# A fused hybrid decoder layer: four plain feed-forward pairs in place of five, six of their eight weight splits kept for the second token half, h2 kept whole, and the last splits tied into a chain

## The chip, the cores and the metric

The kernel runs on one core of one Trainium2 chip. The metric is the device time of one launch in microseconds (us). Three runs of the kernel before gave 939.48, 940.89 and 943.55 us; the median is 940.89 us. TensorE is called PE, VectorE DVE, ScalarE ACT, GpSimd POOL and SyncE SP, as in the profile.

## The reference, cut to what matters

One layer: a gated mixer (attention, gMLP, projections), and then a SwiGLU feed-forward block on 512 prompt tokens and 8 sample tokens (520 in all), with D_MODEL 1024 and D_FF 2816 (22 tiles of 128). The change lies in the last two lines and in the norm ahead of them.

```python
def trunk_layer(x, c, attend, sgu, w_ada, b_ada, norm1_w, w_in, ..., w_out, norm2_w, w_ffn_in, w_ffn_out):
    ...
    x = x + g1 * (merged @ w_out)
    h2 = rms_norm(x, norm2_w) * (1 + sc2) + sh2
    a, b = jnp.split(h2 @ w_ffn_in, 2, axis=-1)
    x = x + g2 * ((jax.nn.silu(a) * b) @ w_ffn_out)
    return x, att_state, vs
```

## The kernel before

Everything is stored with features on the 128 partitions and the 520 tokens in the free dimension, in two halves of 260 (`HT`). Each float32 operand of a large product is split in two float32r parts: `hi`, a rounding copy made by ACT (L68), and `lo`, the rest, made by DVE (L69). A product then takes three matmuls per block of 128 features (`mm3`, L91 to L93: hi·hi, hi·lo, lo·hi), each 128x128 by 260 columns. A weight tile of 1024x128 against one token half is a `product` of 8 blocks, 24 matmuls.

The whole kernel is a list of jobs. `run()` walks it: `steps()` loads a weight tile with SP, splits it on ACT and DVE into a ring of three buffers for `hi` and three for `lo`, and keeps three splits ahead of the products; after each job `tick()` advances the background tasks (norms, sums) by a piece. What comes out is then ordered per engine by a scheduler with a cost model of its own, so an instruction's place on its engine isn't simply its place in the text. PE has four PSUM banks under the tag `mm`, used in turn; a product can start only when the bank's last reader is done.

The stages that matter here, in order of time:

- The out projection, token half by token half (`out_job`, 8 products each); DVE adds each product to the residual (`residual`, L837, for the second half also `rt` and `xr` on the 8 sample tokens, L841 and L842).
- `norm2(half)`, a background task of each half: squares on ACT, sums mostly on POOL, a sum over features by one PE matmul (`tot`, L296), then Ln, Exp and a Newton step (`rsqrt`), and for each of 8 blocks `modulate`: a product on DVE (L277), h2 `hi` on ACT (L279), h2 `lo` on DVE (L280). For the first half it runs beside the second half's out products, for the second half beside the first half's plain feed-forward products.
- The plain feed-forward tiles (`ffn_job`): `NPRE` = 5 tile pairs, gate and value, first all 10 products of the first token half, then all 10 of the second, each time with its weights loaded and split anew. The gate product goes through Silu on ACT (L905), the value product is multiplied with it on DVE (L908).
- `sums()`, a background task in the second half's plain products: it rebuilds h2 as hi + lo (`whole`, L927), and forms differences of its four quarters (L930); three of them go split into `tt`, and the fourth, `t1`, is written over the second half of the first four blocks of h2 once the plain products have read them (ACT L933, DVE L930).
- The other 17 tiles are pairs (`pair_job`). A pair takes seven part products of 12 matmuls, 84 in all, on sums and differences of weights (formed by POOL in `first`, L974 and L975, and by DVE, L990 and L993) and of h2 quarters, where a plain tile pair takes 4 products, 96 matmuls. The first part of each pair (`start_pair`) stands in the pair before; those of the first pair stand at its own start, 24 matmuls ahead of the first use of `t1`.
- The down projection (`down_job`, 8 output tiles, three k ranges). Its operands are the 22 gated tiles, split by `divide` (also L68 and L69): tiles 0 and 1 during the last pairs, 2 to 7 during the last pair into the space of `tt`, 8 to 15 into that of h2, the rest later. `g` L1031 is the last step of a pair, and it frees the pair's bank `pa`.

Of the kernel before, what the change touches and what calls it, by code (L numbers as in the profile page):

```python
# [1 line left out]

# [8 lines left out]
F32 = mybir.dt.float32  # L11
F32R = mybir.dt.float32r
# [15 lines left out]
TILES = {1: 1, 2: 3}  # L28
# [3 lines left out]
def hybrid_layer(ctx: ExitStack, tc: tile.TileContext, io: dict):  # L32
# [88 lines left out]
    def job(src, fn, n=KD):  # L121

        def prep(raws):
            yield weights(*raws[0])

        def use(ops, after):
            fn(*ops[0])
            yield

        jobs.append(([(src, n)], None, prep, use))  # L130

    def run():
# [6 lines left out]
        def loads():  # L139
            while len(raws) < len(jobs):  # L140
                srcs, first = jobs[len(raws)][:2]
# [7 lines left out]
        def steps():  # L149
            for k, (_, _, prep, _) in enumerate(jobs):  # L150
                loads()
                for op in prep(raws[k]):
# [10 lines left out]
        for k, (_, _, _, use) in enumerate(jobs):  # L163
            parts = use(ops[k], ops[k + 1] if k + 1 < len(jobs) else None)
            n = TILES[len(jobs[k][0])]
            for p in range(n):
# [3 lines left out]
                next(step, None)  # L170
# [102 lines left out]
    def modulate(which, f, x, rstd, c0, c1, hi, lo):  # L273
# [7 lines left out]
                                 in1=hi[:, c0:c1].bitcast(F32), op0=ALU.add, op1=ALU.subtract)  # L281

    def modulate_samples(which, f0, n, x, rstd, h):
# [7 lines left out]
        last_h[0] = split(h[:, fs, TP:T], h[:, f0 + KD : f0 + KD + n, TP:T], t)  # L291

# [539 lines left out]
    xr, h2, xr_all, h2_all = [], [], [], []  # L832
# [11 lines left out]
    def norm2(half):  # L844
# [15 lines left out]
        if half == 0:  # L860
            h2_all.append(slots("h", "h2", 2 * KD, F32R))
            h2.extend((h2_all[0][1][f], h2_all[0][1][KD + f]) for f in range(KD))
            scales(1, 0, KD, n2w)
        else:
            modulate_samples(1, 0, KD, xr_all[0][0], rstd2, h2_all[0][0])
        for f in range(KD):
            modulate(1, f, xr[f], rstd2, half * HT, min(half * HT + HT, TP), *h2[f])
# [24 lines left out]
    gs, pend, mem = {}, {}, {}  # L892
# [7 lines left out]
    def ffn_job(i, which, half):  # L900
        def fn(hi, lo):
            p = product(hi, lo, h2, half)
            if which == 0:
# [6 lines left out]
        job(io["wff"][which * NFF + i], fn)  # L910
# [5 lines left out]
    def sums():  # L916

        early.close()
        tt = ctx.enter_context(tc.tile_pool(name="tt", bufs=1)).tile([P, 3, KD, HT], F32R, tag="tt", name="tt")
        mem["tt"] = tt  # L920
        mem["ys"] = slots("ys", "g8")
# [292 lines left out]
```

## Time and profile before

| what | us |
|---|---|
| median of three runs (lowest, highest) | 940.89 (939.48, 943.55) |
| the profiled execution, its own time | 938.87 |
| its span, first to last instruction | 936.7 |
| PE busy in the span | 910.1 (97%) |
| DVE, ACT, POOL busy | 585.3 (62%), 413.1 (44%), 136.0 (15%) |
| feed-forward and down part, from the first plain product to the end | 570.6 to 936.7 |

The page gives busy time per engine, the span in slices, and the costliest groups. In a timeline row the first number is the start, the second the length, and the bracket is the idle time of the engine just before it with what ended it; matmuls overlap, so the time that one costs is the distance between two starts, not its length.

### The profile page before, as it was taken

Reading aid. Unit: us, or ns where it says so; the run is one execution under the profiler, and the core shown is the slowest. Engines: PE = TensorE matmul, PEld = TensorE weight load, DVE = VectorE, ACT = ScalarE, POOL = GpSimd, SP = SyncE. Lnnn points to the kernel's source line nnn. Section 1 sums busy time; section 2 is a strip of 40 time slices with the busy share of each in tenths; the row PEclk is TensorE's granted clock in tenths of the full one; section 3 lists DMA queues with packets and bytes.
Section 4 is the critical chain, followed back from the end, with each engine's and each line's share of the span. In section 5 each row is a group of like instructions: output and inputs, shape, how many; then the busy total and the mean of one; then the engine's idle time right before and its main releaser. Section 6 shows DMA issues by size and latency. Waiting matters only on the chain. (4 is left out here: it accounts for less than half of the span.)

```text
span 936.7 us, 18863 instructions
## 1 busy us (share of the span) xinstructions
PE 910.1 (97%) x7648; PEld 870.7 (93%) x7648; DVE 585.3 (62%) x1378; ACT 413.1 (44%) x802; POOL 136.0 (15%) x155
## 2 busy tenths in 40 slices
PE   3899999999999999999999999999999999899998
PEld 1699889899898989999999999999999999899998
DVE  6734675746655665643337678998887887742321
ACT  4343443533543443763333356664555556622110
POOL 0000002012102102201000322022343342000000
PEclk9999999999999999999999999999999999999999
DMA  9944436738758636635222654542332332343410
GB/s 358 360 160 136 159 113 230 265 97 301 241 175 255 221 98 180 225 111 161 91 91 90 227 180 156 181 159 91 121 106 91 113 113 91 103 143 95 119 40 23
DMA packets 43030, 146.85 MB, mean 157 GB/s; under 512 B 6456, under 2 KB 7448, under 8 KB 42944
## 3 DMA queue, kind: packets, MB, share of 16 engines
q1 hardware_dynamic: 33840, 114.34, 36.1%
q0 software_dynamic: 8608, 31.20, 10.7%
q8 instruction: 60, 0.98, 0.4%
q14 instruction: 26, 0.21, 0.1%
q10 hardware_dynamic: 496, 0.12, 0.1%
HBM read 137.01 MB, written 8.63 MB: 155 GB/s over the span
## 5 line engine op out<-in xcount | busy, mean ns | idle before, releaser
L91 PE MATMUL ps<-h,hi 128*128 128x260 f32 x1248 | 354.7, 287 | 3.1 <-ACT h L279 2.1
L93 PE MATMUL ps<-h,lo 128*128 128x260 f32 x1248 | 353.4, 285 | 0.6 <-DVE lo L69 0.6
L92 PE MATMUL ps<-h,hi 128*128 128x260 f32 x1248 | 353.3, 284 | 0.3 <-DVE h L280 0.3
L69 DVE TENSOR_TENSOR lo<-raw,hi 128x1024 fp32r<-128x1024 f32 (+2 forms) x213 | 220.0, 1050 | 163.3 <-ACT hi L68 161.1
L68 ACT ACTIVATE hi<-raw 128x1024 fp32r<-128x1024 f32 (+2 forms) x213 | 181.5, 875 | 256.2 <-PE ps L92 215.4
L91 PEld LDWEIGHTS ps<-h,hi 128*128 128x128 f32 x1248 | 233.7, 188 | 14.2 <-issue 9.1
L92 PEld LDWEIGHTS ps<-h,hi 128*128 128x128 f32 x1248 | 234.7, 188 | 3.3 <-issue 2.1
L93 PEld LDWEIGHTS ps<-h,lo 128*128 128x128 f32 x1248 | 234.8, 188 | 3.2 <-issue 1.7
L974 POOL TENSOR_TENSOR s<-raw 128x512 f32<-128x512 f32 x17 | 34.2, 2011 | 147.2 <-DMA raw<-wff 114.3
L953 PE MATMUL pb<-h,hi 128*128 128x260 f32 x136 | 38.9, 286 | 1.8 <-DVE h L930 1.8
L954 PE MATMUL pb<-h,lo 128*128 128x260 f32 x136 | 39.1, 287 | 0.0
L952 PE MATMUL pb<-h,hi 128*128 128x260 f32 x136 | 38.9, 286 | 0.0
L953 PE MATMUL pa<-tt,hi 128*128 128x260 f32 x136 | 38.6, 284 | 0.0
L91 PE MATMUL ps<-gh,hi 128*128 128x260 f32 x128 | 36.2, 283 | 2.5 <-DVE g L1031 2.5
L952 PE MATMUL pa<-tt,hi 128*128 128x260 f32 x136 | 38.6, 284 | 0.0
L954 PE MATMUL pa<-tt,lo 128*128 128x260 f32 x136 | 38.3, 282 | 0.0
L93 PE MATMUL ps<-mh,lo 128*128 128x260 f32 x128 | 36.3, 284 | 0.0
L91 PE MATMUL ps<-mh,hi 128*128 128x260 f32 x128 | 36.2, 283 | 0.0
L92 PE MATMUL ps<-ml,hi 128*128 128x260 f32 x128 | 36.2, 283 | 0.0
L92 PE MATMUL ps<-gh,hi 128*128 128x260 f32 x128 | 36.1, 282 | 0.0
L93 PE MATMUL ps<-gh,lo 128*128 128x260 f32 x128 | 36.1, 282 | 0.0
L837 DVE SCALAR_TENSOR_TENSOR xr<-ps,mod,xr 128x260 f32<-128x260 f32 (+1 forms) x32 | 15.4, 482 | 30.8 <-PE ps L93 29.9
(271 smaller groups left out, 1887.2 us busy)
## 6 DMA issues: line engine op xcount, KB each, us to landing
raw<-win SPq DMA_DIRECT2D x60, 512.0 KB, 6.0
raw<-wff SPq DMA_DIRECT2D x54, 512.0 KB, 3.7
wada<-wada SPq DMA_DIRECT2D x48, 512.0 KB, 6.5
raw<-wout SPq DMA_DIRECT2D x16, 512.0 KB, 3.8
raw<-wfo SPq DMA_DIRECT2D x16, 512.0 KB, 3.7
kt<-ck POOLq DMA_DIRECT2D x8, 512.0 KB, 5.8
qb<-dq POOLq DMA_DIRECT2D x8, 512.0 KB, 6.8
raw<-wpj SPq DMA_DIRECT2D x8, 512.0 KB, 3.9
```

The source lines that it names most:

```text
L68: act.activation(hi, src, AF.Copy)
L69: return dve.tensor_tensor(out=lo, in0=src, in1=hi.bitcast(F32), op=ALU.subtract)
L91: pe.matmul(ps, wh, xh[:, cols], start=(first and i == 0), stop=False)
L92: pe.matmul(ps, wh, xl[:, cols], start=False, stop=False)
L93: last_mm[0] = pe.matmul(ps, wl, xh[:, cols], start=False, stop=(last and i == n - 1))
L837: dve.scalar_tensor_tensor(out=dst[:, c0 : c0 + n], in0=ps[:, :n], scalar=g[:, 0:1], in1=x[:, c0 : c0 + n], op0=ALU.mult, op1=ALU.add)
L952: pe.matmul(ps, hi[:, c], xh, start=(first and k == 0), stop=False, skip_group_check=True)
L953: pe.matmul(ps, hi[:, c], xl, start=False, stop=False, skip_group_check=True)
L954: pe.matmul(ps, lo[:, c], xh, start=False, stop=(k == 3), skip_group_check=True)
L974: pool.tensor_tensor(out=own_slot("s1", i % 2)[:, :512], in0=b[:, :512], in1=b[:, 512:], op=ALU.add)
```

## The change

Four things change. The plain tile pairs go from five to four (`NPRE`), so that there are 18 pairs. Of the eight plain weight tiles, six keep their split halves from the first token half to the second: three (`KEPT_HOME`) in buffers of their own (`keep`, in the space of the pool that the mixer used and that `tt` takes later), three (`KEPT_RING`) by staying in the ring, since no further split is put in until they are used again (`second_use`, and the fifth field of a job). The second half takes the tiles in the order 0, 2, 3, 1, and only tile 1 is loaded and split again. `modulate` writes h2 also whole, by a second activation on ACT (new L300), and `sums` starts from that and no longer adds hi and lo. In `divide` each ACT step and each DVE step is tied behind the one before (`chain_`), so that the tiles come in the order of k.

```diff
-    def weights(raw, n):
-        hi = wp.tile([P, 1024], F32R, tag="hi", name="hi")
-        lo = wp.tile([P, 1024], F32R, tag="lo", name="lo")
+    def weights(raw, n, home=None):
+        hi, lo = home() if home else [wp.tile([P, 1024], F32R, tag=tag, name=tag) for tag in ("hi", "lo")]
...
+    def second_use(fn, ring):
+        def prep(raws):
+            return
+            yield
+        def use(ops, after):
+            fn()
+            yield
+        jobs.append(([], None, prep, use, int(ring)))
...
-                next(step, None)
+                if done_:
+                    next(step, None)
...
+        if whole is not None:
+            act.activation(whole[:, c0:c1], t[:, c0:c1], AF.Identity, bias=sh)
...
+    def keep():
+        if kept.pool is None:
+            early.close()
+            kept.stack = ctx.enter_context(ExitStack())
+            kept.pool = kept.stack.enter_context(tc.tile_pool(name="kp", bufs=3))
+        return [kept.pool.tile([P, 1024], F32R, tag=tag, name="k" + tag) for tag in ("hi", "lo")]
...
+            if half == 0 and place:
+                kept.halves[i, which] = hi, lo
+            elif place:
+                hi, lo = kept.halves.pop((i, which))
             p = product(hi, lo, h2, half)
...
-        todo = [lambda: whole(r[0], 0, 0), lambda: whole(r[1], 4, 0), lambda: whole(r[2], 0, 1),
-                lambda: minus(r[0], r[2], r[0]), lambda: whole(r[3], 4, 1), lambda: minus(r[2], r[3], r[2]),
-                lambda: minus(r[3], r[3], r[0]), lambda: minus(r[1], r[1], r[3])]
-        todo += [lambda j=j: halved(tt[:, j, 0:4], tt[:, j, 4:8], r[3 - j]) for j in range(3)]
+        for step in (lambda: minus(b11, b12, b11), lambda: minus(b12, b22, b12), lambda: minus(b22, b22, b11),
+                     lambda: minus(b21, b21, b22)):
+            with behind(last_lo[0]):
+                step()
+            yield 1
+        while not kept.closed:
+            yield 1
+        tt = ctx.enter_context(tc.tile_pool(name="tt", bufs=1)).tile([P, 3, KD, HT], F32R, tag="tt", name="tt")
+        for j, t in ((0, b22), (1, b12), (2, b21)):
+            with behind(last_lo[0]):
+                halved(tt[:, j, 0:4], tt[:, j, 4:8], t)
+            yield 1
...
-            split(*hl, gs[k])
+            with behind(chain_[0]):
+                chain_[0] = act.activation(hl[0], gs[k], AF.Copy)
+            with behind(chain_[1]):
+                chain_[1] = dve.tensor_tensor(out=hl[1], in0=gs[k], in1=hl[0].bitcast(F32), op=ALU.subtract)
...
-    NPRE = 5
-    for half in range(2):
-        for i in range(NPRE):
-            ffn_job(i, 0, half)
-            ffn_job(i, 1, half)
+    NPRE = 4
+    KEPT_HOME = [(0, 0), (0, 1), (NPRE - 2, 0)]
+    KEPT_RING = [(NPRE - 2, 1), (NPRE - 1, 0), (NPRE - 1, 1)]
+    for half, tiles in ((0, range(NPRE)), (1, [0, NPRE - 2, NPRE - 1, *range(1, NPRE - 2)])):
+        for i in tiles:
+            for which in range(2):
+                ffn_job(i, which, half, "home" if (i, which) in KEPT_HOME else "ring" if (i, which) in KEPT_RING else None)
```

On every engine the instructions up to the second half's out products stand as before. Three places behind them are shown.

First, DVE at the end of the out projection, around the eighth and last residual of the second half (the last row with `128x252` here); `klo` is the split of a kept tile. Before:

```order
L837 SCALAR_TENSOR_TENSOR xr<-ps,mod,xr 128x252
L841 TENSOR_TENSOR rt<-ps,mod 128x8
L280 SCALAR_TENSOR_TENSOR h_6819<-modt,mod,h_6819 128x260
L842 TENSOR_TENSOR xr<-rt,xr 128x8
L69 TENSOR_TENSOR lo<-raw,hi 128x1024
L280 SCALAR_TENSOR_TENSOR h_6819<-modt,mod,h_6819 128x260
L837 SCALAR_TENSOR_TENSOR xr<-ps,mod,xr 128x252
L842 TENSOR_TENSOR xr<-rt,xr 128x8
L841 TENSOR_TENSOR rt<-ps,mod 128x8
```

and now (L70, L294, L297, L858, L862 and L863 are the old L69, L277, L280, L837, L841 and L842):

```order
L70 TENSOR_TENSOR klo<-raw,khi 128x1024
L294 SCALAR_TENSOR_TENSOR modt<-xr,amod,rstd_6772 128x260
L863 TENSOR_TENSOR xr<-rt,xr 128x8
L862 TENSOR_TENSOR rt<-ps,mod 128x8
L70 TENSOR_TENSOR lo<-raw,hi 128x1024
L297 SCALAR_TENSOR_TENSOR h_6819<-modt,mod,h_6819 128x260
L294 SCALAR_TENSOR_TENSOR modt<-xr,amod,rstd_6772 128x260
L297 SCALAR_TENSOR_TENSOR h_6819<-modt,mod,h_6819 128x260
L858 SCALAR_TENSOR_TENSOR xr<-ps,mod,xr 128x252
L70 TENSOR_TENSOR lo<-raw,hi 128x1024
L862 TENSOR_TENSOR rt<-ps,mod 128x8
L297 SCALAR_TENSOR_TENSOR h_6819<-modt,mod,h_6819 128x260 x2
```

Between the residual that stands just ahead of the norm's `rstd` and the eighth residual there are now eight weight splits (five before), and six of the eight L297 (all eight L280 before); the `rt` that frees the bank has one more split ahead of it.

Second, PE behind `tot`, the norm's sum for the second token half. The numbers tell the products apart; the rows left out are further matmuls of the product named last. Before, where `ps_7339` takes the bank of `ps_7183`:

```order
L92 MATMUL ps_7183<-h2_6819,hi_7084 128x260
L296 MATMUL tot_7117<-acc2_6782,ones_85 128x260
L93 MATMUL ps_7183<-h2_6819,lo_7085 128x260
...
L91 MATMUL ps_7224<-h2_6819,hi_7130 128x260
...
L91 MATMUL ps_7265<-h2_6819,hi_7177 128x260
...
L91 MATMUL ps_7306<-h2_6819,hi_7218 128x260
...
L91 MATMUL ps_7339<-h2_6819,hi_7259 128x260
```

and now, where `ps_7362` takes the bank of `ps_7199`:

```order
L92 MATMUL ps_7242<-h2_6819,hi_7143 128x260
L317 MATMUL tot_7130<-acc2_6782,ones_85 128x260
L93 MATMUL ps_7242<-h2_6819,lo_7144 128x260
...
L91 MATMUL ps_7285<-h2_6819,khi_7193 128x260
...
L91 MATMUL ps_7335<-h2_6819,hi_7236 128x260
...
L91 MATMUL ps_7362<-h2_6819,hi_7279 128x260
```

Before, 79 matmuls stand between `tot` and the product that needs the bank whose Silu is behind the norm's Ln and Exp on ACT; now 52 do. The first four products, which were finished one after the other, are now woven into each other, and `tot` stands at the end of the fourth; the first matmul of the fourth stands behind 57 of the first three.

Third, DVE at the end of the last pair. Before:

```order
L1030 TENSOR_TENSOR g<-value,gate 128x260
L69 TENSOR_TENSOR lo<-raw,hi 128x1024
L69 TENSOR_TENSOR h_6819<-g,h_6819 128x520 x2
L69 TENSOR_TENSOR h_6819<-g_7371,h_6819 128x520 x6
L1031 TENSOR_TENSOR g<-pa,gate 128x260
L69 TENSOR_TENSOR tt<-g,tt 128x520 x2
```

and now (L1072, L1073 and L1112 are the old L1030, L1031 and the split in `divide`):

```order
L1072 TENSOR_TENSOR g<-value,gate 128x260
L1112 TENSOR_TENSOR tt<-g,tt 128x520
L70 TENSOR_TENSOR lo<-raw,hi 128x1024
L1073 TENSOR_TENSOR g<-pa,gate 128x260
L1112 TENSOR_TENSOR tt<-g,tt 128x520 x2
L1112 TENSOR_TENSOR h_6819<-g,h_6819 128x520 x2
L1112 TENSOR_TENSOR h_6819<-g_6820,h_6819 128x520 x6
```

The eight splits of gated tiles 8 to 15 now stand behind the last step of the pair and behind tiles 6 and 7.

## Rows read from the trace of the kernel before

**Rows 1.** The page, part 1: busy time and share by engine.

```profile
PE 910.1 (97%) x7648; PEld 870.7 (93%) x7648; DVE 585.3 (62%) x1378; ACT 413.1 (44%) x802; POOL 136.0 (15%) x155
```

**Rows 2.** Waits of PE: waiter, whom for; us in total, times, longest.

```profile
PE ps L91 <- DVE g L1031: 2.5, 1, 2.5
...
PE pb L953 <- DVE h L930: 1.8, 1, 1.8
```

**Rows 3.** Busy by stretch: us, PE, PEld, DVE, ACT, POOL, clock, DMA share, GB/s.

```profile
600.00:625.00 25.00, 25.00 (x210) 24.84 (x210) 25.00 (x27) 14.20 (x18) 3.95 (x2) 1.00 0.58 192
625.00:640.00 15.00, 13.20 (x98) 13.00 (x97) 13.39 (x19) 7.13 (x15) 4.38 (x4) 0.89 0.30 107
```

**Rows 4.** Timeline of POOL in the pairs (start, length, instruction, idle before).

```profile
659.33 2.82 POOL L974 TENSOR_TENSOR s<-raw 128x512 f32<-128x512 f32 x1 [6.62 <-DVE al L69]
...
699.66 2.88 POOL L974 TENSOR_TENSOR s<-raw 128x512 f32<-128x512 f32 x1 [6.56 <-DVE al L69]
```

**Rows 5.** Timeline of PE at the first use of t1.

```profile
631.78 0.28 PE L952 MATMUL pb<-h,hi 128*128 128x260 f32 x1
633.86 0.43 PE L953 MATMUL pb<-h,hi 128*128 128x260 f32 x1 [1.80 <-DVE h L930]
...
637.33 0.36 PE L953 MATMUL pa<-tt,hi 128*128 128x260 f32 x1
637.53 0.28 PE L954 MATMUL pa<-tt,lo 128*128 128x260 f32 x1
```

**Rows 6.** Timeline of DVE ahead of t1.

```profile
625.22 3.49 DVE L69 TENSOR_TENSOR lo<-raw,hi 128x512 fp32r<-128x512 f32 x2
...
629.23 0.68 DVE L990 TENSOR_TENSOR raw<-s,raw 128x512 f32<-128x512 f32 x1
...
632.58 1.23 DVE L930 TENSOR_TENSOR h<-g,h 128x1040 fp32r<-128x1040 f32 x1
633.73 1.28 DVE L69 TENSOR_TENSOR lo<-raw,hi 128x512 fp32r<-128x512 f32 x2
```

**Rows 7.** Timeline of POOL in the same stretch.

```profile
625.18 1.29 POOL L974 TENSOR_TENSOR s<-raw 128x512 f32<-128x512 f32 x1 [2.45 <-DMA raw<-wff]
626.54 1.61 POOL L975 TENSOR_TENSOR raw<-raw 128x512 f32<-128x512 f32 x1
```

**Rows 8.** Timeline of ACT in the same stretch.

```profile
629.95 0.63 ACT L68 ACTIVATE hi<-raw 128x512 fp32r<-128x512 f32 x1 [2.63 <-DVE raw L990]
630.48 1.06 ACT L933 ACTIVATE h<-g 128x1040 fp32r<-128x1040 f32 x1
```

**Rows 9.** Timeline of PE at the end of the last pair.

```profile
810.38 0.52 PE L91 MATMUL ps<-tt,hi 128*128 128x260 f32 x3
813.37 0.39 PE L91 MATMUL ps<-gh,hi 128*128 128x260 f32 x1 [2.46 <-DVE g L1031]
```

**Rows 10.** Timeline of DVE at the same place.

```profile
808.01 4.96 DVE L69 TENSOR_TENSOR h<-g,h 128x520 fp32r<-128x520 f32 x8
812.89 0.42 DVE L1031 TENSOR_TENSOR g<-pa,gate 128x260 f32<-128x260 f32 x1
```

**Rows 11.** Timeline of ACT: the second half's norm between two Silu.

```profile
577.53 1.28 ACT L905 ACT_TABLE_LOAD   x1
...
586.28 0.39 ACT L905 ACTIVATE silu<-ps 128x260 f32<-128x260 f32 x1
```

**Rows 12.** Timeline of PE: the first plain product, and just behind tot.

```profile
570.60 0.28 PE L91 MATMUL ps<-h,hi 128*128 128x260 f32 x1
...
578.65 0.47 PE L93 MATMUL ps<-h,lo 128*128 128x260 f32 x1
```

**Rows 13.** Timeline of DVE: the eighth residual of the second half.

```profile
573.67 0.47 DVE L837 SCALAR_TENSOR_TENSOR xr<-ps,mod,xr 128x252 f32<-128x252 f32 x1
...
574.21 1.21 DVE L69 TENSOR_TENSOR lo<-raw,hi 128x1024 fp32r<-128x1024 f32 x1
```

**Rows 14.** Timeline of ACT: h2 hi of the first half.

```profile
560.15 1.71 ACT L279 ACTIVATE h<-modt,mod 128x260 fp32r<-128x260 f32 x4
```

More of the change, by code (lines that the diff above doesn't have):

```diff
@@ L149, in steps @@
         def steps():
-            for k, (_, _, prep, _) in enumerate(jobs):
+            for k, (srcs, _, prep, _, _) in enumerate(jobs):
                 loads()
+                if not srcs:
+                    ready[0] = k + 1
+                    loads()
                 for op in prep(raws[k]):
@@ L271, in scales, with modulate @@
                                  .to_broadcast([P, n // 2, 2, 9]), op0=ALU.add, op1=ALU.mult)
-    def modulate(which, f, x, rstd, c0, c1, hi, lo):
+    def modulate(which, f, x, rstd, c0, c1, hi, lo, whole=None):
         sh = sh_sc(which, f)[0][:, 0:1]
@@ L291, in modulate_samples @@
         last_h[0] = split(h[:, fs, TP:T], h[:, f0 + KD : f0 + KD + n, TP:T], t)
+        if whole is not None:
+            act.activation(whole[:, fs, TP:T], t, AF.Copy)
     def total(sq, tag):
@@ L898, in home, with ffn_job, fn @@
         return gs[i]
-    def ffn_job(i, which, half):
-        def fn(hi, lo):
+    kept = SimpleNamespace(pool=None, closed=False, halves={})
+    def keep():
[4 more added lines that the diff above has]
+        return [kept.pool.tile([P, 1024], F32R, tag=tag, name="k" + tag) for tag in ("hi", "lo")]
+    def ffn_job(i, which, half, place=None):
+        def fn(hi=None, lo=None):
+            if half == 0 and place:
+                kept.halves[i, which] = hi, lo
+            elif place:
+                hi, lo = kept.halves.pop((i, which))
             p = product(hi, lo, h2, half)
+            if half and place == "home" and not kept.halves.keys() & set(KEPT_HOME):
+                kept.stack.close()
+                kept.closed = True
             if which == 0:
@@ L908, in fn, with minus @@
             dve.tensor_tensor(out=home(i)[:, c], in0=p, in1=pend[i], op=ALU.mult)
-        job(io["wff"][which * NFF + i], fn)
+        if half and place:
+            second_use(fn, place == "ring")
+        else:
+            job(io["wff"][which * NFF + i], fn, home=keep if place == "home" else None, again=(place == "ring"))
     def sums():
[L918 to L921, printed above, removed]
-        r = [mem["ys"][0][:, 2 * j : 2 * j + 2].rearrange("p a (b c) -> p (a b) c", b=2) for j in range(4)]
-        def whole(out, k0, half):
-            c = slice(half * HT, half * HT + HT)
-            h = h2_all[0][0].bitcast(F32)
-            dve.tensor_tensor(out=out, in0=h[:, k0 : k0 + 4, c], in1=h[:, KD + k0 : KD + k0 + 4, c], op=ALU.add)
-        def minus(out, a, b):
-            dve.tensor_tensor(out=out, in0=a, in1=b, op=ALU.subtract)
+        b = mem["ys"][0]
+        b11, b12, b21, b22 = b[:, 0:4, 0:HT], b[:, 0:4, HT:T], b[:, 4:8, 0:HT], b[:, 4:8, HT:T]
+        def minus(out, x, y):
+            dve.tensor_tensor(out=out, in0=x, in1=y, op=ALU.subtract)
         def halved(hi, lo, src):
```

32 lines of the change are left out of this document (18 added, 14 removed).

## The prediction

> **What bounds the kernel now.** I read the page's busy shares first, then PE's waits, then PE's timeline around each wait, and last what DVE, ACT and POOL did there. PE is busy for 97% of the span [rows 1], so time goes only where matmuls go, or where PE stands idle or slow. What a matmul costs is read from the pairs: POOL starts the same step of a pair at 659.33 and, four pairs on, at 699.66 [rows 4]; 40.33 us over 4 x 84 matmuls is 0.120 us each. In the part that the change touches PE waits twice for long [rows 2].
>
> The first is at t1. The matmul at 631.78 should have been followed at 631.90, and was at 633.86 [rows 5]: 1.96 us. Behind it 17 matmuls take 3.67 us (633.86 to 637.53), where 0.120 each makes 2.04: 1.63 us more. The mean granted clock of 625 to 640 is 0.89 [rows 3], so for a part of it PE ran at the lower of its two levels, 1.2 in place of 2.4 GHz, right behind the wait. Together 3.6 us. Why was t1 late? The last plain product ended 24 matmuls before 631.78, at 628.9, but ACT began t1 at 630.48, behind a weight split that waited for DVE's L990 [rows 8]. DVE reached L990 at 629.23 [rows 6], since it had no idle time (25.00 of 25 us [rows 3]), and since two steps of 512 columns took 3.49 us beside POOL's two [rows 7], where the same form takes 1.28 without POOL [rows 6]: 2.2 us lost.
>
> The second is behind the last pair: 2.46 us until DVE's L1031 is done and the bank `pa` is free [rows 9]. DVE had put eight splits, 4.96 us, ahead of that step [rows 10].
>
> **The change part by part.** Sums are made against the profiled execution's own 938.87 us (span 936.7, and 2.17 around it); the median of the runs is 2.02 higher, and I carry the difference over to it.
>
> *One plain pair becomes a bridged one.* 96 matmuls become 84: 12 x 0.120 = 1.44 us less on PE. The splits that this pair needs on ACT and DVE lie beside PE, as those of the other 17 do; the rows show no wait of PE inside the pairs. So -1.44.
>
> *The t1 wait.* In the second half's plain products DVE had ten splits and four `whole` steps; now two splits and none. At 1.21 us a split [rows 13] and 1.23 a step of 1040 columns [rows 6] that is 14.6 us less DVE work, while the stretch gets shorter by two products, 48 matmuls, 5.8 us. DVE thus gets some 9 us of air. From the last plain product's end to t1's first use there are still 24 matmuls, 2.88 us; t1 itself takes 1.06 on ACT and 1.23 on DVE [rows 6, 8], 2.3. It fits if both engines come to it in time. What stays: ACT's split ahead of t1 still waits for L990, and POOL's work on the second pair still falls just ahead, because its load waits for a raw buffer that tile 1's split frees. Bounds: 0 (all in time) and the 1.96 of [rows 5]. I take 0.3, near the lower end, as only POOL's share of the lateness is left and the backlog is not. With so short a wait the slow stretch goes too. Gain 1.96 + 1.63 - 0.3 = 3.3.
>
> Here a rule of the Trainium skill speaks against the change. The row says that DVE lost 2.2 us to 2.9 us of POOL work [rows 6, 7]. The page "SBUF — State Buffer", section "SBUF: two separate sides", says that the port pair which VectorE and GpSimd share is an exclusive lock held for the whole instruction, so that the other blocks fully. By the row L990 slips by 2.2 us, by the rule by up to 2.9; with the latter t1 would be some 0.7 us later still, which is a wait of about 1 us in place of 0.3.
>
> *The end of the last pair.* L1031 now stands ahead of the eight splits, so the bank comes free 4.96 us earlier than before, and the whole 2.46 goes. What is late next? Tiles 6 and 7: behind the pair's last matmul PE has 25 matmuls (3.0 us) that need neither, and DVE needs 0.42 and two splits of 0.62, a good 1.7 us. Tiles 8 to 15: first needed after 58 matmuls, 7.0 us, and done by then (0.42 + 10 x 0.62 = 6.6), in the order in which they are read. So -2.46; bounds 0 and -2.46, as a tie to the chain could cost it.
>
> *h2 whole, and kept splits ahead of time.* Kept tiles need no ring slot, so their splits come earlier: three more splits stand ahead of the eighth residual, and two modulate steps fewer. 3 x 1.21 less 2 x 0.47 (the price of the residual, a step of the same form [rows 13]) is 2.7 us: the residual starts at 573.67 + 2.7 = 576.4, and `rt`, which frees its bank, stands behind another split: 576.4 + 0.47 + 1.21 = 578.1. PE wants that bank for the fourth plain product, after 57 matmuls from 570.60 [rows 12]: 577.4. A wait of 0.7, with POOL's additions in the same time a little more; I take 0.9. Bounds: 0, and 2.7 if nothing on PE were left to cover the shift.
>
> *The norm of the second half.* On ACT, the Silu that frees the third product's bank stands behind two table loads, Ln and Exp and DVE's Newton steps. In the trace that runs from just ahead of 578.65, where `tot` ends [rows 12], to 586.28 + 0.39 = 586.67 [rows 11]: 8.0 us. PE had 79 matmuls, 9.5 us, and didn't wait. Now it has 52, 6.2 us. The chain has the same links (one split fewer, and the first Silu closer behind), so a wait of 8.0 - 6.2 = 1.8; I take 1.7. Bounds: 0, if the chain is shorter by the split and more, and 3.2 by counting from the first table load's start at 577.53 [rows 11], 9.1 us. What queues behind: ACT's h2 steps for the second half, which PE needs only four products later.
>
> The six loads and splits that go (eight with the fifth pair's) weren't waited for. The 16 new ACT steps of 0.43 each [rows 14] lie beside PE except as counted above.
>
> *Sum:* -1.44 - 3.3 - 2.46 + 0.9 + 1.7 = -4.6. Against 938.87 that is 934.3; carried to the median, 940.89 - 4.6 = **936.3 us**.
>
> **The rivals.**
>
> *A slow stretch behind a new wait.* In [rows 5] a wait of 1.96 us left 1.63 us of matmuls at the lower clock. For it: two new waits of 0.9 and 1.7. Against it: the 2.46 of [rows 9] left none of note. Price +1.6: 937.9.
>
> *The t1 wait stays*, by POOL's lock as above, with L990 and ACT's split in the same order as before. For it: order and POOL's place are the same. Against it: DVE's backlog is gone. Price 3.3: 939.6.
>
> *The new waits don't show.* For it: the scheduler wove the first products together to keep PE at work, and POOL and ACT may run better than the rows. Against it: the counts 79 and 52. Price -2.6: 933.7.
>
> *Slower than before:* the front of the feed-forward part, overloaded. ACT gets 8 x 0.43 = 3.4 us of whole steps and DVE 3 x 1.21 = 3.6 us of splits in the stretch that already had a saturated DVE. If both lie on one chain (residual, modulate, h2), the first plain products start 7.0 late in place of 2.7. It decides from the point where the lateness passes what 57 matmuls cover; the forecast is already 0.9 beyond it, and each us more costs a us. Price: 7.0 - 0.9 = 6.1 and a slow stretch of 1.6, +7.7: 944.0. Against it: each whole step stands behind the h2 step of its block, and no residual waits for it; only DVE's share lies on the chain.
>
> **How the numbers follow.** Chances: the forecast 0.48 (its own range 934.8 to 937.8), slow stretch 0.17, t1 stays 0.13, no new waits 0.15, slower 0.05, and 0.02 for several at once. The range that holds 8 in 10 reaches down to a little below 933.7 and up past 939.6: 932.5 to 940.3. A measurement of this kernel tells about 0.5%, 4.7 us, from no change: below 936.2 is faster, over 945.6 slower. The forecast lies on that edge, so it gives half of itself, 0.24; with 0.15 of the case without new waits and 0.04 from the low ends of the others, faster is 0.43. Slower needs more than the overload's 944.0: 0.04. The rest, 0.53, is within.
>
> **What would show it.** In the changed kernel's profile: no wait of PE on L1073 (the old L1031) behind the last pair; at t1 less than 1 us and matmuls 0.12 apart behind it; new waits of PE at the start of the plain products, one on DVE's L862 (the eighth residual's `rt`), one on ACT's Silu some 50 matmuls behind `tot`; `tt` and `divide` steps on DVE with idle time between them; 12 matmuls fewer. Wrong would be: a wait at t1 as long as before, a new wait for h2 in the second token half, or a wait in the down products for a split tied into the chain.

## The result and the profile after

| kernel | median us (lowest, highest; runs) | ratio to the kernel before, 95% interval |
|---|---|---|
| before, in the same group of runs | 940.18 (937.05, 943.55; 6) | |
| changed | 933.43 (932.87, 934.58; 6) | 0.9943 [0.9924, 0.9963] |
| before, beside the first four experiments | 938.22 (936.13, 941.73; 29) | |
| changed, beside them | 934.02 (933.2, 934.72; 5) | 0.995 [0.9934, 0.9966] |

The profiled execution took 932.99 us (span 931.1), where that of before took 938.87 (span 936.7). Of these 5.6 us of span 1.2 arose ahead of the change: the matmul behind the first half's `tot` starts at 551.53 where it stood at 552.70 before, though the instructions up to there are the same. Over the profiles of all kernels here that `tot` starts anywhere from 551.23 to 553.91 us, so this part belongs to the execution. Some 4.4 us are left for the change; the prediction said 4.6.

The changed kernel's page, busy time and share by engine, beside [rows 1]:

```profile
PE 909.2 (98%) x7636; PEld 869.0 (93%) x7636; DVE 580.4 (62%) x1376; ACT 414.8 (45%) x818; POOL 137.6 (15%) x157
```

Twelve matmuls fewer. Its waits of PE, beside [rows 2] (waiter, whom for; us in total, times, longest): the waits on L1031 (now L1073) and on t1 are not in the list; two new ones are, both named ahead. The rows between them lie ahead of the change.

```profile
PE ps L91 <- ACT silu L946: 1.3, 1, 1.3
...
PE ps L91 <- DVE rt L862: 0.2, 1, 0.2
```

Busy by stretch, beside [rows 3] (us, PE, PEld, DVE, ACT, POOL, clock, DMA share, GB/s):

```profile
600.00:625.00 25.00, 24.79 (x205) 24.37 (x204) 21.45 (x26) 13.49 (x22) 3.23 (x2) 1.00 0.17 56
625.00:640.00 15.00, 15.00 (x128) 15.00 (x127) 13.04 (x18) 7.38 (x15) 6.47 (x4) 1.00 0.32 120
```

DVE has air ahead of t1 (21.45 of 25 us, 25.00 before), and the clock is 1.00 behind it (0.89 before). The timeline of PE at the four places (start, length, instruction, idle before), beside [rows 5, 9, 12]:

```profile
576.74 0.28 PE L91 MATMUL ps<-h,hi 128*128 128x260 f32 x1
577.17 0.36 PE L91 MATMUL ps<-h,hi 128*128 128x260 f32 x1 [0.16 <-DVE rt L862]
...
581.71 0.48 PE L93 MATMUL ps<-h,lo 128*128 128x260 f32 x1
...
588.25 0.28 PE L93 MATMUL ps<-h,lo 128*128 128x260 f32 x1
589.80 0.39 PE L91 MATMUL ps<-h,hi 128*128 128x260 f32 x1 [1.27 <-ACT silu L946]
...
621.52 0.28 PE L994 MATMUL pb<-h,hi 128*128 128x260 f32 x1
621.95 0.39 PE L995 MATMUL pb<-h,hi 128*128 128x260 f32 x1
...
623.47 0.28 PE L995 MATMUL p<-h,hi 128*128 128x260 f32 x1
623.82 0.39 PE L994 MATMUL pa<-tt,hi 128*128 128x260 f32 x1
...
807.29 0.52 PE L91 MATMUL ps<-tt,hi 128*128 128x260 f32 x3
807.65 0.28 PE L91 MATMUL ps<-gh,hi 128*128 128x260 f32 x1
```

Read from start to start, less the 0.12 of a matmul: 0.31 us at `rt`, 1.43 at the Silu, 0.31 at t1 and 0.23 at the gate step just behind it, and none at the end of the last pair. DVE at the same places, beside [rows 6, 10, 13]:

```profile
575.18 0.47 DVE L858 SCALAR_TENSOR_TENSOR xr<-ps,mod,xr 128x252 f32<-128x252 f32 x1
575.57 1.38 DVE L70 TENSOR_TENSOR lo<-raw,hi 128x1024 fp32r<-128x1024 f32 x1
576.88 0.15 DVE L862 TENSOR_TENSOR rt<-ps,mod 128x8 f32<-128x8 f32 x1
...
613.63 2.39 DVE L70 TENSOR_TENSOR lo<-raw,hi 128x512 fp32r<-128x512 f32 x2
615.95 1.78 DVE L70 TENSOR_TENSOR al<-raw,ah 128x512 fp32r<-128x512 f32 x1
617.65 0.68 DVE L1032 TENSOR_TENSOR raw<-s,raw 128x512 f32<-128x512 f32 x1
...
620.66 1.23 DVE L966 TENSOR_TENSOR h<-g,h 128x1040 fp32r<-128x1040 f32 x1
...
805.57 0.43 DVE L1073 TENSOR_TENSOR g<-pa,gate 128x260 f32<-128x260 f32 x1 [1.21 <-PE pa L996]
...
807.13 4.97 DVE L1112 TENSOR_TENSOR h<-g,h 128x520 fp32r<-128x520 f32 x8
```

The residual starts at 575.18 and `rt` at 576.88, 1.2 us earlier than I worked out (576.4 and 578.1); the whole front is that much earlier. L1073 now waits for PE, not PE for it. POOL and ACT around t1, and ACT's chain behind `tot`, beside [rows 7, 8, 11]:

```profile
613.87 1.61 POOL L1016 TENSOR_TENSOR s<-raw 128x512 f32<-128x512 f32 x1 [20.86 <-DMA raw<-wff]
615.55 1.62 POOL L1017 TENSOR_TENSOR raw<-raw 128x512 f32<-128x512 f32 x1
```

```profile
582.43 1.28 ACT L200 ACT_TABLE_LOAD   x1
583.73 2.01 ACT L69 ACTIVATE hi<-raw 128x1024 fp32r<-128x1024 f32 x2
...
588.07 1.28 ACT L946 ACT_TABLE_LOAD   x1 [1.57 <-DVE ms L209]
589.36 0.39 ACT L946 ACTIVATE silu<-ps 128x260 f32<-128x260 f32 x1
...
618.36 0.63 ACT L69 ACTIVATE hi<-raw 128x512 fp32r<-128x512 f32 x1 [1.55 <-DVE raw L1032]
618.90 1.06 ACT L969 ACTIVATE h<-g 128x1040 fp32r<-128x1040 f32 x1
```

From the matmul that stands with `tot` (581.71) to the product behind the Silu (589.80) it is 8.1 us; I had read 8.0 from before.

Where the time went, by two stretches of PE: from the start of the first half's `tot` to that of the last pair's last part product, before 255.66 us (552.46 to 808.12), now 253.96 (551.29 to 805.25); from there to the end of the span 128.58 and 125.85. So 1.70 came from the first, 2.73 from the second.

### The profile page after: what moved, and what is told of

It reads as the page before. It is cut to its first block, busy times and chain, and to the rows that moved or that the text cites. A ratio compares the mean times of both kernels' runs of the same rounds, so it can differ in the third digit from the quotient of the medians.

```text
span 931.1 us, 18828 instructions
## 1 busy us (share of the span) xinstructions
PE 909.2 (98%) x7636; PEld 869.0 (93%) x7636; DVE 580.4 (62%) x1376; ACT 414.8 (45%) x818; POOL 137.6 (15%) x157
## 4 chain that ended last, share of the span: by engine, by line
PE 91%; DVE 3%; DMA 2%; ACT 2%; issue 1%; ACTq 0%; DVEq 0%; SPq 0%
PE ps L91 21%; PE ps L92 20%; PE ps L93 20%; PE pa L994 4%; PE pa L995 4%; PE pa L996 4%; PE ada L259 2%; PE pb L996 2%; PE pb L995 2%; PE pb L994 2%; PE y L672 1%; DMA wada<-wada 1%; PE ssq L524 1%; DVE lo L70 1%; PE p L996 1%
## 5 line engine op out<-in xcount | busy, mean ns | idle before, releaser
L91 PE MATMUL ps<-h,hi 128*128 128x260 f32 x1168 | 333.2, 288 | 4.0 <-ACT h L296 1.6
L93 PE MATMUL ps<-h,lo 128*128 128x260 f32 x1168 | 331.6, 285 | 0.5 <-DVE lo L70 0.5
L92 PE MATMUL ps<-h,hi 128*128 128x260 f32 x1168 | 331.3, 284 | 0.0
L70 DVE TENSOR_TENSOR lo<-raw,hi 128x1024 fp32r<-128x1024 f32 (+2 forms) x205 | 207.7, 1030 | 160.9 <-ACT hi L69 158.4
L69 ACT ACTIVATE hi<-raw 128x1024 fp32r<-128x1024 f32 (+2 forms) x205 | 170.7, 857 | 232.0 <-PE ps L92 203.1
L91 PEld LDWEIGHTS ps<-h,hi 128*128 128x128 f32 x1168 | 219.0, 189 | 16.0 <-issue 9.4
L93 PEld LDWEIGHTS ps<-h,lo 128*128 128x128 f32 x1168 | 220.3, 189 | 2.8 <-issue 1.7
L92 PEld LDWEIGHTS ps<-h,hi 128*128 128x128 f32 x1168 | 220.0, 188 | 2.8 <-issue 2.1
L995 PE MATMUL pb<-h,hi 128*128 128x260 f32 x144 | 40.8, 283 | 0.1
L994 PE MATMUL pa<-tt,hi 128*128 128x260 f32 x144 | 40.8, 283 | 0.1
L995 PE MATMUL pa<-tt,hi 128*128 128x260 f32 x144 | 40.8, 283 | 0.0
L994 PE MATMUL pb<-h,hi 128*128 128x260 f32 x144 | 40.7, 282 | 0.0
L996 PE MATMUL pa<-tt,lo 128*128 128x260 f32 x144 | 40.6, 282 | 0.0
L858 DVE SCALAR_TENSOR_TENSOR xr<-ps,mod,xr 128x260 f32<-128x260 f32 (+1 forms) x32 | 15.4, 483 | 30.7 <-PE ps L93 29.9
```

The source lines that it names most:

```text
L69: act.activation(hi, src, AF.Copy)
L70: return dve.tensor_tensor(out=lo, in0=src, in1=hi.bitcast(F32), op=ALU.subtract)
L91: pe.matmul(ps, wh, xh[:, cols], start=(first and i == 0), stop=False)
L92: pe.matmul(ps, wh, xl[:, cols], start=False, stop=False)
L93: last_mm[0] = pe.matmul(ps, wl, xh[:, cols], start=False, stop=(last and i == n - 1))
L858: dve.scalar_tensor_tensor(out=dst[:, c0 : c0 + n], in0=ps[:, :n], scalar=g[:, 0:1], in1=x[:, c0 : c0 + n], op0=ALU.mult, op1=ALU.add)
```

## The experiments

The first four ran on one chip and share its runs of the kernel before (938.22 us); the chain alone, the copied gate product and the two kernels with tile 1 on another (937.68); the chain's repeat and the two that change the number of pairs on a third (938.46); the second profile of the kernel before on a fourth (937.84). "First stretch" and "second stretch" are the two just named. The yardstick is the run that comes first, the changed kernel on the first of these chips; a median compared with it from another chip also holds the difference between the chips.

**The change again**, as a yardstick.

> The changed kernel as it is, as the yardstick of its companions. Theory (waits): the change pays 1.44 us by 12 matmuls, and the rest by two waits of PE that go (at t1, with a slow stretch behind it, and behind the last pair) less two that come at the front of the plain products. So the profile shows again a wait of 1.2 to 1.7 us on a Silu some 52 matmuls behind tot, under 0.5 us at t1, none behind the last pair; time 0.5% to 0.7% below the kernel before. Rival (less work): the gain is that ACT, DVE and the DMA queues have less to do everywhere, and no single wait carries it.

934.02 us. The waits came at the same places with the same lengths (0.33, 1.43, 0.29); first stretch 254.18, second 125.84.

**Without the chain.**

```diff
-            with behind(chain_[0]):
-                chain_[0] = act.activation(hl[0], gs[k], AF.Copy)
-            with behind(chain_[1]):
-                chain_[1] = dve.tensor_tensor(out=hl[1], in0=gs[k], in1=hl[0].bitcast(F32), op=ALU.subtract)
+            split(*hl, gs[k])
```

> The changed kernel with the last splits not tied into a chain. In the order that comes out, DVE has the eight splits of tiles 8 to 15 (8 x 0.62 us) ahead of the last pair's L1073 again. Theory (waits): PE waits 2.3 to 2.9 us behind the last pair for L1073, as in the kernel before, and nothing else moves: time 2.3 to 2.9 us over the changed kernel's. Rival (less work): the same instructions are done, so the time stays within 0.5 us.

936.94 us (12 runs), 2.9 above the yardstick; span 2.3 above. Its PE timeline at the end of the last pair:

```profile
808.69 0.52 PE L91 MATMUL ps<-tt,hi 128*128 128x260 f32 x3
811.17 0.39 PE L91 MATMUL ps<-gh,hi 128*128 128x260 f32 x1 [1.96 <-DVE g L1073]
```

The wait is back, and all else is as in the yardstick. First stretch 253.85, where the yardstick has 254.18. The order that the chain forces is the gain, not less work.

**All eight tiles loaded and split twice**; h2 whole and the chain stay. No kept split holds the space of `tt` any more, so `tt` doesn't wait for it.

```diff
-        while not kept.closed:
-            yield 1
+        early.close()
...
-    for half, tiles in ((0, range(NPRE)), (1, [0, NPRE - 2, NPRE - 1, *range(1, NPRE - 2)])):
-        for i in tiles:
+    for half in range(2):
+        for i in range(NPRE):
             for which in range(2):
-                ffn_job(i, which, half, "home" if ... else "ring" if ... else None)
+                ffn_job(i, which, half)
```

> The changed kernel with four plain pairs whose eight tiles are all loaded and split again for the second token half, in the order 0 to 3; h2 whole and the chain stay. Theory (waits): six splits more on DVE (6.8 us) in the second half bring the t1 wait back, 1.5 to 2.5 us, perhaps with a slow stretch of some 1.6; at the front, where no split comes ahead of its turn, 79 matmuls stand behind tot again and both new waits are gone, 1.7 us less. In sum 0 to +1 us against the changed kernel without a slow stretch, up to +2.5 with one. Rival (less work): six loads and splits more on DVE, ACT and SP cost their share everywhere: 3 us or more, with small waits all over the second half.

936.01 us (11 runs), 2.0 above the yardstick. Its waits of PE behind 570 us:

```profile
PE pb L994 <- DVE h L966: 1.9, 1, 1.9
PE ps L93 <- DVE lo L70: 0.5, 2, 0.4
```

Both front waits are gone, and the t1 wait stands again. The t1 wait is 2.14 us from start to start, less 0.12, and no slow matmuls stand behind it. So the kept splits do both: they free DVE ahead of t1, and, made ahead of time, they crowd the front. They exchange one wait for another. What the exchange is worth is less clear: 2.0 us by the medians, but the first stretch of this profile is 254.97, only 0.8 over the yardstick's, and the second is the same.

**h2 whole by DVE in place of ACT**: four sums hi + lo in `sums`, as before the change, two steps per tick.

```diff
-            act.activation(whole[:, c0:c1], t[:, c0:c1], AF.Identity, bias=sh)
+            pass
...
-        for step in (lambda: minus(b11, b12, b11), ...
+        for n, step in enumerate((lambda: rebuilt(b11, 0, 0), lambda: rebuilt(b12, 0, 1), lambda: minus(b11, b12, b11), ...
...
```

> The changed kernel with h2 rebuilt as hi + lo by four DVE steps of 1.24 us in the second half, two steps of the sums to a tick so that they still fit, in place of the 16 ACT steps. Theory (waits): kept tiles leave DVE air enough for the four steps, so the t1 wait stays under 0.7 us; the front's waits stay, since they come from the kept tiles' early splits, and its order is another one: 55 matmuls behind tot, a wait on the Silu of 1.5 to 4 us, and 1 to 2 on the eighth residual's rt. In sum +0.5 to +3 us against the changed kernel, all of it at the front. Rival (less work): 16 ACT steps (6.9 us) go and 4 DVE steps (5 us) come; if DVE is what binds, the t1 wait is back at 2 us or more and the front is unchanged.

939.04 us (12 runs), 5.0 above the yardstick. The busy shares of its stretch 585 to 600, and DVE in it:

```profile
585.00:600.00 15.00, 11.35 (x75) 11.14 (x74) 13.63 (x25) 7.66 (x15) 2.69 (x2) 0.78 0.21 71
```

```profile
588.63 2.38 DVE L976 TENSOR_TENSOR g<-h 128x1040 f32<-128x1040 f32 x2
...
591.39 1.37 DVE L209 SCALAR_TENSOR_TENSOR ms<-rs_t,ms 128x260 f32<-128x260 f32 x1
```

The t1 wait is about the yardstick's (0.34 us). The cost is at the front, and the first stretch is 260.05, 5.9 over the yardstick's. The wait on `rt` is 1.84 us from start to start, less 0.12 (0.33 in the yardstick):

```profile
576.06 0.36 PE L91 MATMUL ps<-h,hi 128*128 128x260 f32 x1 [1.68 <-DVE rt L862]
```

And two of the sum steps stand ahead of the norm's Newton steps, and two of these take 1.37 us each where the changed kernel has 0.43, since they now fall beside POOL's steps of the first pair (591.11, 1.36 us, and 592.55, 1.33); the Silu came so much later that PE waited 3.81 us beyond the 0.12, and behind it stand 25 matmuls 0.22 us apart. In this kernel, not in the changed one, the prediction's rival "slow stretch behind a new wait" came, and with it an overload of the front, though by the sum steps and not by the chain of steps that the prediction named.

**The chain alone**, in the kernel before, on two chips.

```diff
-            split(*hl, gs[k])
+            with behind(chain_[0]):
+                chain_[0] = act.activation(hl[0], gs[k], AF.Copy)
+            with behind(chain_[1]):
+                chain_[1] = dve.tensor_tensor(out=hl[1], in0=gs[k], in1=hl[0].bitcast(F32), op=ALU.subtract)
```

> The kernel before with one part of the change alone: the steps of divide tied in a chain by k; five pairs, no kept splits. Theory (each long wait has its own cause, and what an edit gives is the wait that it removes): PE's wait for DVE's last g step (2.46 us in the profile before) goes whole, the wait at t1 (1.96 us and what it leaves of slow matmuls) stays, no wait at the front; 2.3 to 2.9 us faster than the kernel before, ratio 0.9969 to 0.9976. Rival (the gain of the chain needs the four pairs: with the backlog of splits at the end of the last pair as before, the chain only shifts it): the wait moves to the down products that read tiles 8 to 15, 1 us or more there, and the gain is under 1.5 us.

934.63 against 937.68 us, ratio 0.9961 [0.9947, 0.9976]: 3.05 us, somewhat over the range; first stretch 253.86, second 125.84. It needs nothing else of the change. At t1 its PE timeline shows the wait of before, but not the slow matmuls behind it:

```profile
631.11 0.28 PE L952 MATMUL pb<-h,hi 128*128 128x260 f32 x1
633.12 0.40 PE L953 MATMUL pb<-h,hi 128*128 128x260 f32 x1 [1.73 <-DVE h L930]
633.35 0.28 PE L954 MATMUL pb<-h,lo 128*128 128x260 f32 x1
```

> The chain alone in the kernel before, once more: its first profile had the t1 wait (2.01 us) with matmuls 0.12 us apart behind it, where the kernel before had 0.22 for 17 matmuls behind the same wait. Theory (the stretch at the lower clock behind a wait of about 2 us comes in some executions and not in others, and the 1.63 us that I gave to it is a part of the gain in some runs only): t1 wait 1.9 to 2.1 us again, with or without 0.22 per matmul behind it; runs with a mean granted clock of 0.996 are 1 to 2 us longer than those with 0.999 or 1.0; median 2 to 3.5 us below the kernel before. Rival (it is the end wait that decides it, or the amount of DVE work, so the stretch never comes in this kernel): matmuls 0.12 apart, all runs within 0.8 us.

935.16 against 938.46 us, ratio 0.9968 [0.9956, 0.9979]. The t1 wait is 1.96 us, again with 0.12 per matmul behind it; first stretch 254.46. The runs lie 2.5 us apart, against the rival's 0.8; those with a mean clock of 1.0 took 933.76, 934.92 and 935.03, the one with 0.996 took 935.76. That points the theory's way, but is too little to show it.

**The kernel before, profiled once more.**

> The kernel before itself, a second profile of it. Theory (the stretch at the lower clock is a matter of the execution, not of the kernel): the waits at t1 and on L1031 are there again, 1.9 to 2.1 and 2.4 to 2.6 us between starts beyond 0.12; behind one or both, or neither, matmuls stand 0.22 apart, and not in the same places as in the first profile; from the first half's tot to the last part product it takes 254.0 to 254.6 us without such a stretch (255.66 with the one behind t1 in the first profile). Rival (the stretch behind the t1 wait belongs to this kernel, for DVE's backlog or the splits there): 17 or so matmuls at 0.22 behind t1 again, 255.5 us or more.

Its PE timeline at t1 and at the end of the last pair:

```profile
632.52 0.39 PE L952 MATMUL pb<-h,hi 128*128 128x260 f32 x1
634.78 0.39 PE L953 MATMUL pb<-h,hi 128*128 128x260 f32 x1 [1.88 <-DVE h L930]
...
635.12 0.28 PE L952 MATMUL pb<-h,hi 128*128 128x260 f32 x1
635.24 0.28 PE L953 MATMUL pb<-h,hi 128*128 128x260 f32 x1
...
809.75 0.52 PE L91 MATMUL ps<-tt,hi 128*128 128x260 f32 x3
812.74 0.39 PE L91 MATMUL ps<-gh,hi 128*128 128x260 f32 x1 [2.46 <-DVE g L1031]
```

A wait of 2.14 us and no slow matmul behind it; the end wait is 2.63 us, also without. First stretch 254.40, where the first profile had 255.66. The theory holds: the 1.63 us of [rows 5] belongs to an execution, not to the kernel. And the same kernel, put on one chip twice (two loads), gave 940.46 us (8 runs) and 937.84 (9 runs), ratio 1.0022 [1.0008, 1.0036]: between two loads the median alone moves by 2.6 us, outside such an interval.

**Tile 1's gate product copied out of its bank ahead of Silu.**

```diff
                 pend[i] = slot("tr", "silu", shape=(P, HT))
+                if half == 0 and i == 1:
+                    act.activation(pend[i], p, AF.Copy)
+                    p = pend[i]
```

> The changed kernel; the gate product of tile 1, first token half, is copied out of its bank by ACT ahead of its Silu (1 more ACT step of some 0.4 us), so that the bank's release does not stand behind the norm's Ln and Exp. Theory (the norm's chain on ACT, not the single bank, is what is late; PE runs out of other work behind it): PE's wait of 1.43 us on this bank goes, and a wait of about as much appears at the next thing that stands behind the same chain, the value product's bank, whose product with the Silu waits for it: time within 0.5 us of the changed kernel, 933.5 to 934.5. Rival (the bank alone is the wait): 1.4 us less than the changed kernel, no wait of PE over 0.5 us between tot and t1.

933.49 us. The Silu wait is gone, and its like stands one product later (waits of PE):

```profile
PE ps L91 <- DVE g L952: 1.3, 1, 1.3
```

1.42 us beyond the 0.12 there. Not the one bank is late, but the norm's chain on ACT, as the theory said.

**Own buffers for tile 1 in place of tile 0**, so that these splits come later; and the same with **both products of tile 1 copied out** (gate by ACT as above, value by DVE).

```diff
-    KEPT_HOME = [(0, 0), (0, 1), (NPRE - 2, 0)]
+    KEPT_HOME = [(1, 0), (1, 1), (NPRE - 2, 0)]
...
-    for half, tiles in ((0, range(NPRE)), (1, [0, NPRE - 2, NPRE - 1, *range(1, NPRE - 2)])):
+    for half, tiles in ((0, range(NPRE)), (1, [1, NPRE - 2, NPRE - 1, 0])):
```

> The changed kernel; the buffers of their own go to tile 1 in place of tile 0, and the second half takes the tiles in the order 1, 2, 3, 0: kept splits that are made later in the front part, so that fewer of them stand ahead of the eighth residual on DVE. Theory (splits put ahead of the eighth residual cause the wait on rt): the wait on rt (0.3 us over the usual distance) goes, the Silu wait stays at 1.0 to 1.5 us, t1 is as in the changed kernel; 0.3 to 1.2 us faster than the changed kernel: 932.8 to 933.7. Rival (rt is late for POOL's additions in the same stretch, not for the splits): no change, 934.0; or tile 0's second load, now last, comes late and PE waits for it, 1 us or more, slower.

932.82 us (930.65 to 935.0): the wait on `rt` is gone, the Silu wait is 1.01, tile 0's second load is not late. The median alone tells little against the changed kernel's 933.43 and 934.02; the first stretch, 252.45, is 1.5 to 1.7 us shorter than in its two profiles.

> As home1, and both products of tile 1 in the first token half are copied out of their banks (gate by ACT, value by DVE) ahead of Silu and of the product with it: neither bank stands behind the norm's Ln and Exp. Theory (the norm's chain is late for the banks first and for h2 of the second half after that, which is needed some 24 to 50 matmuls later): the Silu wait goes; of its 1.4 us some part, 0 to 1, comes back as a wait for h2 of the second half (ACT's or DVE's modulate steps); time 0.5 to 1.5 us below home1, 931.8 to 933.2. Rival (h2 of the second half is as late as the banks): no gain over home1, with a wait of 1.2 us or more on a modulate step of the second half.

931.69 us (930.93 to 932.77), ratio to before 0.9926 [0.9907, 0.9945]: below both kernels. Neither front wait is left:

```profile
575.00:600.00 25.00, 24.94 (x207) 24.68 (x206) 21.88 (x43) 17.03 (x35) 5.34 (x5) 1.00 0.37 119
```

PE was busy for 23.57 us of 575 to 600 in the changed kernel, here for 24.94. First stretch 251.62, 2.3 us under the changed kernel's. With 2.6 us between two loads of one kernel, the medians alone wouldn't prove that against the changed kernel (933.49 to 934.02 in these groups); the stretch and the missing waits do.

**Five pairs again** in the changed kernel.

```diff
-    NPRE = 4
+    NPRE = 5
```

> The changed kernel with five plain pairs again (the same six splits kept, so tiles 1 and 2 are split twice). Theory (the twelve matmuls cost 0.120 each; PE finds 49 matmuls behind tot instead of 52 ahead of the bank that waits for the Silu; more plain products give DVE air ahead of t1): 1.44 for matmuls, 0.3 to 1.2 more at the Silu, 0 to 0.5 less at t1: 1.2 to 2.6 us slower than the changed kernel, 934.8 to 936.4. Rival (a pair less is worth less than its matmuls, since a bridged pair's splits fall on ACT and DVE where they are late): within 0.5 us of the changed kernel or below it, 933 to 934.2.

937.79 us (12 runs), 3.8 above the yardstick: the direction was right, the size was not. Its longest waits of PE behind 570 us, and DVE and ACT behind `tot`:

```profile
PE ps L91 <- ACT silu L946: 3.2, 2, 2.7
```

```profile
587.22 3.50 DVE L70 TENSOR_TENSOR lo<-raw,hi 128x1024 fp32r<-128x1024 f32 x3 [1.61 <-ACT hi L69]
```

```profile
591.34 1.06 ACT L69 ACTIVATE hi<-raw 128x1024 fp32r<-128x1024 f32 x1 [1.64 <-PE ps L92]
```

Three weight splits stand in the norm's chain on DVE, and on ACT four, where the changed kernel has two each; the fourth, which stands just ahead of the second Silu, came only after ACT had waited 1.64 us for PE. From start to start, less 0.12, the waits are 0.78 and 2.89 us, and behind the second stand matmuls 0.22 us apart. The first stretch is 258.34, 4.2 over the yardstick's: 1.44 for the matmuls, and the longer waits and the slow matmuls less what is gone (the wait on `rt`, and half of that at t1). The expectation had only the count of 49 matmuls for the Silu, and not what else the new order puts into the norm's chain.

**Four pairs alone**, in the kernel before, its sums two steps per tick.

```diff
-        for step in todo:
+        for n, step in enumerate(todo):
...
-            yield 1
+            if n % 2:
+                yield 1
...
-    NPRE = 5
+    NPRE = 4
```

> The kernel before with four plain pairs and nothing else of the change, but that its sums take two steps per tick, since eight products leave too few ticks for one (all weights split twice, h2 not whole, no chain). Theory (DVE had no time left at t1 with ten products to work beside; with eight it is later by the work that it can't shift): 1.44 us of matmuls less, the wait on L1031 stays (2 to 2.5), waits at t1 or on splits ahead of it 3 us or more longer in sum than the 1.96 before: 0.5 to 6 us slower than the kernel before, 938.5 to 944. Rival (the matmuls are what the change gives, the kept splits are not needed for it): 1 to 2 us faster than the kernel before, with a t1 wait of at most 2.3 us.

946.0 us, ratio 1.0075 [1.006, 1.009]: 7.5 us slower, beyond even the range. Its waits of PE behind 570 us:

```profile
PE pb L954 <- DVE h L930: 2.5, 1, 2.5
PE ps L91 <- DVE g L1032: 2.4, 1, 2.4
PE ps L91 <- ACT silu L905: 2.0, 1, 2.0
```

Right behind the waits on the Silu and on L1032, and 2.3 us behind the one on t1, stand runs of matmuls 0.22 us apart, three in one profile. The first stretch is 261.37, 7.0 over that of the kernel before without a slow stretch. The pair that saves 1.44 us of matmuls, put in without the rest and with the sums packed closer, costs five times that.

## Why the prediction was right, and where not

The forecast was 936.3 us, a gain of 4.6; measured 933.43, inside the range, and 4.4 us in the profile behind the point where the kernels begin to differ. The median lies below the forecast's own range (934.8 to 937.8) and beside the 933.7 of the rival "the new waits don't show"; but both new waits are in the profile, so that rival is not what happened. Between medians the gain is 6.8 us in the first group of runs and 4.2 in the second. Term by term:

- *One plain pair less, -1.44.* Twelve matmuls went.
- *The end of the last pair, -2.46.* Shown from both sides: the second stretch is 2.73 us shorter, by the chain alone too (125.84), and without the chain the wait returns. The term was some 0.27 too small: I read the idle time of [rows 9], and from start to start, less 0.12 a matmul, the same wait is 2.63 with another 0.1 behind it.
- *The t1 wait, 1.96 less 0.3.* 0.31 was left at t1 and 0.23 more at the gate step behind it, which I hadn't listed. The causes were the two named: DVE's backlog is gone (with six splits more on DVE the wait is back), and ACT's split still waits for the step that POOL delays; besides, DVE's own t1 step stood behind two more splits until 620.66, 0.7 us after ACT's was done. Taken together with POOL's two steps, three DVE steps took 4.02 us (613.63 to 617.65) where they take 0.60 each without POOL: 2.2 lost. POOL's two took 3.2, but one alone takes 1.29 (L1017 at 689.43, DVE idle), so of the 3.2 some 0.6 is POOL's own delay, and 2.6 its work. The rule of the Trainium skill that I weighed ("SBUF — State Buffer", section "SBUF: two separate sides"), a port lock for whole instructions, would take up to these 2.6. The trace is not far from that, and a small DVE step (L309, 128x64, at 591.78) took 1.32 us beside a POOL step of 1.36, where it takes 0.22 without one (five pairs, 595.72). So the rows don't settle the rule; the wait of about 1 us that I worked out by it did not come.
- *The slow stretch behind t1, -1.63.* This is the step that was wrong: "With so short a wait the slow stretch goes too" is true of the execution profiled before, but a second profile of the same kernel has the wait and no such stretch, and so have both of the chain alone. I counted a part of one execution as a part of the kernel. Without it the first stretch falls by 0.4 us (254.40 to 253.96), not by 1.7, and the whole sum would have been 3.0, where the second profile of before gives 0.4 and 2.8 for the two stretches. That the forecast of 4.6 met the 4.4 of the profiles is thus in part luck: the profile it was compared with was the one that had the slow stretch.
- *The wait on `rt`, +0.9.* 0.31, the front being somewhat earlier than worked out. The cause is the one predicted: with tile 1 kept in place of tile 0 it goes.
- *The Silu wait, +1.7.* 1.43, by the count of 52 matmuls against a chain of 8.1 us, nearly as worked out. (The upper bound there was added up wrongly: 9.1 less 6.2 is 2.9, not 3.2; nothing hangs on it.)
- *Missed:* four gaps of 0.23 to 0.28 us between matmuls of the out projection at 563.80 to 564.78, 0.5 us in sum, and restarts of 0.1 behind each wait. What causes the first wasn't tried; the yardstick has three such gaps there. Of the signs named ahead one didn't come: on DVE the eight `divide` steps stand back to back (4.97 us from 807.13), and no wait of PE followed from it.

So apart from the chain the change hardly pays: beside the second profile of before, the matmuls and t1 give 3.0 us (1.44, and 2.14 less the 0.54 that is left), and as the first stretch falls by 0.4 only, the new front waits (1.74) and small gaps take 2.6 back. Even the 0.4 is no more than executions differ by: with the chain alone the first stretch was 253.86 and 254.46, with the whole change 253.96 and 254.18. By the medians the rest beside the chain is worth about 1 us (4.2 for the change, 3.05 to 3.3 for the chain alone), which is less than two loads of one kernel differ by; that it gains anything isn't shown. What was expected from it is found again when the front is relieved: the version with tile 1 kept and both its products copied out has a first stretch 2.8 us under that of before without the slow stretch.

The absolute time was predicted 2.9 us too high, mostly for another reason: I carried the gain to 940.89, the median of three runs, but other groups of runs of that kernel have medians of 937.68 to 940.46. The profiled execution's own 938.87 less 4.6, 934.3, was nearer. The rivals: the t1 wait did not stay, and no slow stretch followed the new waits in the profile of the changed kernel or its repeat. An overload of the front did come with h2 whole by DVE, by other steps: 5.0 us over the changed kernel, where I had 7.7 over the forecast for it.

What stays open: why two loads of one kernel differ by 2.6 us, and why the runs of the kernel before spread over 5.6 us (936.13 to 941.73) where those of the changed one spread over 1.5 (29 runs against 5). Of 62 runs of before, the ten with a mean clock of 1.0 took 936.8 us on average, the 41 with 0.996 to 0.998 took 938.9. Stretches at the lower clock behind its two long waits would fit; in which places they fell in those runs no profile shows.

## What to carry to other kernels

Ask of a change in an ordered kernel not only which wait it removes but how many matmuls then stand between each bank's release and its next use: the counts 79 and 52 gave the new wait to 0.3 us. The count alone isn't enough: where the new order also put further steps into the chain that the bank waits for, 49 and 55 matmuls came with waits of 2.89 and 3.81 us. Try the parts alone and left out: here they add up in neither way (one part alone gains 3 us, another alone loses 7.5, and each left out costs 2 to 5 by the medians). Before a stall's after-effects are booked as a gain, look at a second profile of the same kernel.

## What the runs showed of the hardware

- A stretch at the lower clock behind a wait of PE is not a fixed price of the wait. Waits, from start to start less 0.12, of 2.63 us (before, end, in both profiles), 2.14 (second profile of before, and all tiles split twice, t1), 2.12 (without the chain, end), 1.89 and 1.96 (chain alone) left none; the first profile's 1.96 left 17 matmuls at 0.22 us, 2.21 and 2.57 (four pairs alone, Silu and end) left them too, as did 2.89 (five pairs) and 3.81 (h2 whole by DVE, 25 matmuls).
- A lower mean clock need not cost anything. The changed kernel has a granted clock of 0.89 from 15 to 30 us, its repeat has 1.00 there; the first half's `tot` started at 551.29 and 552.28. Over all fourteen profiles, six have 0.89 or 0.90 in that stretch, and their `tot` starts at 552.6 on average; the eight with 1.00 have 552.5. In that stretch the DMA engines are fully busy (the row of the changed kernel's windows):

```profile
15.00:30.00 15.00, 12.20 (x112) 6.60 (x104) 12.84 (x38) 7.49 (x16) 0.00 (x0) 0.89 1.03 417
```
